# A decoder trunk on one core: one embedding projected later, one transposed earlier

## The chip, the cores and the metric
The kernel runs on one NeuronCore of a Trainium2 chip. The metric is the device time of one execution in microseconds (us). The kernel before takes 2688.65 us, the median of three timed runs (2688.11 to 2694.91).

## The reference
The program computes a decoder trunk of two layers on 256 tokens of width 2048, in float32. Each layer ends with a small product of an embedding `p[i]` (256 tokens by 256) and a weight of 256 by 2048, which enters only in the layer's last line:

```python
for i in range(DEPTH):                       # DEPTH = 2
    mix = ...                                # even: RWKV-7 and window attention; odd: differential attention
    x = layer_norm(alpha * x + mix, ln1_g[i], ln1_b[i])                                # first norm
    x = layer_norm(alpha * x + swiglu(x, ffn_w1[i], ffn_w3[i], ffn_w2[i]), ln2_g[i], ln2_b[i])  # second norm
    x = x + jax.nn.sigmoid(x @ ple_w_gate[i]) * (p[i] @ ple_w_proj[i])
```

So the product of `p[i]` and `ple_w_proj[i]` depends on nothing that the layer computes, and it may be done at any time before the gate is applied.

## The kernel before
The 256 tokens lie in two tiles of 128 rows (`x[0]`, `x[1]`), each 128 by 2048. A product is kept near float32 accuracy by splitting both factors in a high and a low half (`hi`/`lo` of a weight, `x0h`/`x0l` and so on of the activations) and adding three matmuls of 128x128 by 128x512: high by high (line 133), high by low (134), low by high (135).

`gemm` makes 512 columns of a product: two accumulators, one for each token tile, each a PSUM bank from the pool `mm` of four. Its weights come from `split_weights`: SP's queue loads 128x2x512 (512 KB, `raw`, four buffers), ACT makes `hi` (line 109), DVE makes `lo` (line 110); there are six `hi`/`lo` slots after `more()`. One such weight tile feeds 12 matmuls: two halves, three terms, two token tiles. A full product over x has eight weight tiles and 96 matmuls; the argument `head=HEAD` lets the first four tiles of a product run for the first token tile before they run for the second.

A norm is `ln_finish`. For each of four column groups (c) and both token tiles (t), DVE normalises in two operations (lines 221 and 223), PE transposes four blocks of 128x128 into a PSUM tile of the pool `sm` (line 229, in two pairs), and ACT and DVE split each pair in halves (lines 176 and 177) into `x0h`, `x0l`, ..., `x7l`. The FFN (`ffn`) follows a first norm: in two parts (six and five groups of 512 columns) it makes the products with w1 and w3, SiLU and transposes, and then the product with w2. `ple` follows a second norm: the gate's product, the sigmoid, and the sum.

The embedding goes through `embed` (load p), `embed_t` (transpose to `pTh`, `pTl`, by `split_t`, lines 170, 176, 177) and `project` (product with `ple_w_proj`, four groups of 512 columns, of one weight tile and 12 matmuls each, copied to `pj` by ACT in line 291). Before the change each layer projects groups 0 and 1 behind its first norm and groups 2 and 3 behind its second. The buffers of p and of pT are single, so those of layer 1 reuse those of layer 0.

The order in which an engine runs its instructions is fixed when the kernel is built, and it isn't the order of the code: the framework's scheduler moves an instruction ahead of others on its engine. An engine then runs its row strictly as it stands there, and waits at an instruction whose inputs are missing.

Of the kernel before, what the change touches and what calls it, by code (L numbers as in the profile page):

```python
# [47 lines left out]
class Trunk:  # L48
# [195 lines left out]
                nc.vector.bn_stats(out=st[t][:, c], in_=xc)  # L244


    def ffn(self, x, xT, w1, w3, w2):
        nc = self.nc
        st = self.ln_start()
        with self.tc.tile_pool(name="ffn", bufs=1) as fp:  # L250
            k0 = 0
            for part, chunks in enumerate((range(0, 6), range(6, 11))):
                gT = []
                for c in chunks:
                    h1 = self.gemm(xT, w1, c * 512, head=HEAD if c == 0 else 0)
                    sl = []
                    for t in range(NT):
                        s = fp.tile([P, 512], F32, name="silu", bufs=3)
                        nc.scalar.activation(out=s, in_=h1[t], func=AF.Silu)
                        sl.append(s)  # L260
                    h3 = self.gemm(xT, w3, c * 512)
                    for t in range(NT):
                        nc.vector.tensor_tensor(out=sl[t], in0=sl[t], in1=h3[t], op=ALU.mult)
                    for j in range(2):
                        gT.append(self.split_t([sl[t][:, j * 256:(j + 1) * 256] for t in range(NT)],
                                               f"g{len(gT)}", fp))
                for c in range(4):
                    acc = self.gemm(gT, w2, c * 512, rows=range(k0, k0 + 2 * len(gT), 2),
                                    tail=TAIL if part == 1 and c == 3 else 0)
                    self.residual(x, acc, c, st, first=part == 0, last=part == 1)  # L270
                k0 += 2 * len(gT)
        return st


    def embed(self, p):

        pt = []
        for t in range(NT):
            pc = self.ep.tile([P, PLE], F32, name=f"p{t}")
            self.nc.sync.dma_start(out=pc, in_=p[t * P:(t + 1) * P])  # L280
            pt.append(pc)
        return pt

    def embed_t(self, pt):
        return [self.split_t(pt, "pT", self.ep)]

    def project(self, pT, wpj, chunks, pj):
# [71 lines left out]
def kview(w):  # L359
    return w.rearrange("(ko p) n -> p ko n", p=P)  # L360
# [637 lines left out]
@with_exitstack  # L998
def decoder_trunk(ctx: ExitStack, tc: tile.TileContext, out, stop=None, **a):
    nc = tc.nc  # L1000
    T = Trunk(ctx, tc)
    T.ident = T.cp.tile([P, P], F32, name="ident")
    make_identity(nc, T.ident)
    T.mhalf = T.const("mhalf", [P, 4], -0.5)
    T.ninf = T.const("ninf", [P, 1], -3e38)

    def dump(x):
        for t in range(NT):
            nc.sync.dma_start(out=out[0, t * P:(t + 1) * P], in_=x[t])

    for i in range(DEPTH):
        p, wpj = a["p"][i, 0], kview(a["ple_w_proj"][i])
        if i % 2 == 0:
            x, st = even_layer(T, a, a["x"][0])
            T.more()
            T.ln_begin(a["ln1_g"][i], a["ln1_b"][i])
            pt = T.embed(p)
            banks = T.psum(4, 4)
        else:
            banks = T.psum(4, 4)  # L1020
            xT = T.transpose_x(x)
            T.ln_begin(a["ln1_g"][i], a["ln1_b"][i])
            pt = T.embed(p)
            st = odd_layer(T, x, xT, a, i)
        with tc.tile_pool(name="pj", bufs=1) as jp:
            pj = [jp.tile([P, D], F32, name=f"pj{t}") for t in range(NT)]
            xT = T.ln_finish(x, st)
            T.ln_begin(a["ln2_g"][i], a["ln2_b"][i])
            if stop == (i, 1):
                banks.close()  # L1030
                return dump(x)
            pT = T.embed_t(pt)
            T.project(pT, wpj, (0, 1), pj)
            st = T.ffn(x, xT, kview(a["ffn_w1"][i]), kview(a["ffn_w3"][i]), kview(a["ffn_w2"][i]))
            xT = T.ln_finish(x, st)
            if stop == (i, 2):
                banks.close()
                return dump(x)
            T.project(pT, wpj, (2, 3), pj)
            T.ple(x, xT, pj, kview(a["ple_w_gate"][i]), out[0] if i == DEPTH - 1 else None)  # L1040
        banks.close()
        if stop == (i, 3):
            return dump(x)
# [20 lines left out]
```

## Time and profile before

| | us |
|---|---|
| median of three timed runs | 2688.65 |
| lowest, highest | 2688.11, 2694.91 |
| the profiled execution | 2683.93 |
| its span, first to last instruction | 2682.2 |
| PE busy in it | 2595.9 (97%) |
| DVE, ACT busy | 1494.3, 1142.2 |
| granted TensorE clock, mean | 0.977 |

The granted clock is a share of 2.4 GHz, and 0.50 is the lower level of 1.2 GHz. PE is TensorE's matmul row, PEld its weight loads. Lines are those of the kernel before. The matmuls overlap at their ends, so the distance from one start to the next says what one costs.

### The profile page before, as it was taken

How to read it: one execution, taken by the hardware profiler on the slowest of the kernel's cores; microseconds unless marked ns; L12 is line 12 of the kernel's file. 1: busy time of each engine (PE TensorE's matmuls, PEld its weight loads, DVE VectorE, ACT ScalarE, POOL GpSimd, SP SyncE). 2: the span in 40 equal slices, each digit the busy share in tenths (PEclk: the TensorE clock that was granted, in tenths of full speed). 3: DMA queues.
4: the chain of work that ended last, by engine and by line, in shares of the span. 5: the costliest groups of instructions: out<-in, count | busy, mean ns of one | idle time of the engine just before them, and what ended most of it. 6: DMA issues, size and time to landing. Idle time of an engine off the chain costs nothing.

```text
span 2682.2 us, 32574 instructions
## 1 busy us (share of the span) xinstructions
PE 2595.9 (97%) x12509; PEld 2101.7 (78%) x12509; DVE 1494.3 (56%) x2072; ACT 1142.2 (43%) x1493; POOL 122.8 (5%) x190
## 2 busy tenths in 40 slices
PE   8998799989999999999999999998999999999999
PEld 6877566768888888888788777786888888888877
DVE  4769536674545444545666555555545444545574
ACT  5443224544444334444444454444444434444343
POOL 0113421000000000000000000000000000000000
PEclk9989889989999999999999999998999999999999
DMA  6335312556666666666575555555666666666654
GB/s 189 110 108 149 95 40 78 174 168 201 188 189 188 195 191 192 188 190 190 173 226 180 163 158 165 166 183 154 188 190 188 192 191 194 189 189 188 195 175 164
DMA packets 240282, 458.56 MB, mean 171 GB/s; under 512 B 15280, under 2 KB 20066, under 8 KB 240126
## 3 DMA queue, kind: packets, MB, share of 16 engines
q1 hardware_dynamic: 240126, 456.48, 56.4%
q8 instruction: 98, 1.61, 0.2%
q14 instruction: 58, 0.48, 0.1%
HBM read 453.28 MB, written 2.10 MB: 170 GB/s over the span
## 4 chain that ended last, share of the span: by engine, by line
PE 88%; DVE 6%; POOL 2%; DMA 2%; ACT 1%; issue 1%; SPq 0%; POOLq 0%; ACTq 0%; DVEq 0%
PE acc L133 26%; PE acc L134 25%; PE acc L135 25%; DVE lo L110 1%; PE acc L155 1%; PE acc L159 1%; PE acc L157 1%; PE s L170 1%; PE s L229 1%; DMA raw<-in_e_w_in_dram 1%; PE sx L861 1%; ACT hi L109 1%; DVE blk L609 0%; PE s L730 0%; DVE lmat L708 0%
## 5 line engine op out<-in xcount | busy, mean ns | idle before, releaser
L110 DVE TENSOR_TENSOR lo<-raw,hi 128x1024 fp32r<-128x1024 f32 (+2 forms) x840 | 1023.6, 1220 | 990.3 <-ACT hi L109 987.7
L109 ACT CAST hi<-raw 128x1024 fp32r<-128x1024 f32 (+2 forms) x840 | 879.0, 1047 | 1215.0 <-PE acc L135 1095.2
L133 PE MATMUL acc<-hi,x0h 128*128 128x512 f32 (+1 forms) x292 | 119.1, 408 | 0.3 <-ACT x0h L176 0.3
L134 PE MATMUL acc<-lo,x3h 128*128 128x512 f32 (+1 forms) x292 | 114.9, 394 | 4.3 <-DVE lo L110 4.3
L135 PE MATMUL acc<-hi,x0l 128*128 128x512 f32 (+1 forms) x292 | 117.3, 402 | 0.0
L134 PE MATMUL acc<-lo,x2h 128*128 128x512 f32 (+1 forms) x292 | 114.9, 393 | 2.3 <-DVE lo L110 2.3
L133 PE MATMUL acc<-hi,x1h 128*128 128x512 f32 (+1 forms) x292 | 116.9, 400 | 0.0
L134 PE MATMUL acc<-lo,x6h 128*128 128x512 f32 (+1 forms) x292 | 114.2, 391 | 2.2 <-DVE lo L110 2.2
L134 PE MATMUL acc<-lo,x4h 128*128 128x512 f32 (+1 forms) x292 | 114.5, 392 | 1.4 <-DVE lo L110 1.4
L135 PE MATMUL acc<-hi,x1l 128*128 128x512 f32 (+1 forms) x292 | 115.8, 396 | 0.0
L134 PE MATMUL acc<-lo,x1h 128*128 128x512 f32 (+1 forms) x292 | 115.7, 396 | 0.0
L133 PE MATMUL acc<-hi,x4h 128*128 128x512 f32 (+1 forms) x292 | 114.4, 392 | 1.2 <-DVE x L242 1.2
L134 PE MATMUL acc<-lo,x0h 128*128 128x512 f32 (+1 forms) x292 | 115.5, 396 | 0.0
L133 PE MATMUL acc<-hi,x2h 128*128 128x512 f32 (+1 forms) x292 | 115.3, 395 | 0.0
L133 PE MATMUL acc<-hi,x3h 128*128 128x512 f32 (+1 forms) x292 | 115.0, 394 | 0.0
L134 PE MATMUL acc<-lo,x5h 128*128 128x512 f32 (+1 forms) x292 | 114.1, 391 | 0.8 <-DVE lo L110 0.8
L135 PE MATMUL acc<-hi,x3l 128*128 128x512 f32 (+1 forms) x292 | 114.8, 393 | 0.0
L135 PE MATMUL acc<-hi,x7l 128*128 128x512 f32 (+1 forms) x292 | 114.7, 393 | 0.0
L135 PE MATMUL acc<-hi,x2l 128*128 128x512 f32 (+1 forms) x292 | 114.7, 393 | 0.0
L134 PE MATMUL acc<-lo,x7h 128*128 128x512 f32 (+1 forms) x292 | 114.6, 393 | 0.0
L133 PE MATMUL acc<-hi,x7h 128*128 128x512 f32 (+1 forms) x292 | 114.1, 391 | 0.0
L133 PE MATMUL acc<-hi,x6h 128*128 128x512 f32 (+1 forms) x292 | 113.9, 390 | 0.0
(561 smaller groups left out, 5196.3 us busy)
## 6 DMA issues: line engine op xcount, KB each, us to landing
raw<-in_ffn_w_dram SPq DMA_DIRECT2D x528, 512.0 KB, 3.7
raw<-in_o_w_in_dram SPq DMA_DIRECT2D x96, 512.0 KB, 3.9
raw<-in_e_w_in_dram SPq DMA_DIRECT2D x64, 512.0 KB, 3.6
raw<-in_ple_w_gate_dram SPq DMA_DIRECT2D x64, 512.0 KB, 4.6
raw<-in_e_w_out_dram SPq DMA_DIRECT2D x32, 512.0 KB, 3.6
raw<-in_o_w_out_dram SPq DMA_DIRECT2D x32, 512.0 KB, 4.1
x<-in_x_dram SPq DMA_DIRECT2D x16, 256.0 KB, 5.1
lng<-in_ln_g_dram SPq DMA_DIRECT2D x16, 256.0 KB, 3.2
```

The costliest lines, as they stand in the source:

```text
L109: nc.scalar.copy(out=hi, in_=raw)
L110: nc.vector.tensor_tensor(out=lo, in0=raw, in1=hi.bitcast(F32), op=ALU.subtract)
L133: nc.tensor.matmul(o, xh[:, kk, s], hi[:, kk], start=k == 0, stop=False)
L134: nc.tensor.matmul(o, xh[:, kk, s], lo[:, kk], start=False, stop=False)
L135: nc.tensor.matmul(o, xl[:, kk, s], hi[:, kk], start=False, stop=k == 2 * n - 1)
L155: nc.tensor.matmul(o, hi[:, kk, fs], xh[:, kk], start=k == 0 and i % 2 == 0, stop=False, skip_group_check=True)
L157: nc.tensor.matmul(o, lo[:, kk, fs], xh[:, kk], start=False, stop=False, skip_group_check=True)
L159: nc.tensor.matmul(o, hi[:, kk, fs], xl[:, kk], start=False, stop=k == nk - 1, skip_group_check=True)
L170: nc.tensor.transpose(ps[:, kk, t * P:(t + 1) * P], src[t][:, kk * P:(kk + 1) * P], self.ident)
L229: nc.tensor.transpose(ps[:, 2 * j + kk], x[t][:, f:f + P], self.ident)
L861: nc.tensor.matmul(ps, qT[s, c, f % 4, t * P:(t + 1) * P], kT[c][s, 0:nk * P], start=True, stop=True)
```

## The change
`embed_t` is gone: `embed` now loads and transposes. Layer 0 calls it between the FFN's two parts, and projects all four groups behind its second norm and none behind its first. Layer 1 calls it at the layer's start, before the attention, and projects as before (0 and 1 behind the first norm, 2 and 3 behind the second).

```diff
-    def ffn(self, x, xT, w1, w3, w2):
+    def ffn(self, x, xT, w1, w3, w2, between=None):
...
                     self.residual(x, acc, c, st, first=part == 0, last=part == 1)
                 k0 += 2 * len(gT)
+                if part == 0 and between:
+                    between()
         return st
...
             pt.append(pc)
-        return pt
-
-    def embed_t(self, pt):
         return [self.split_t(pt, "pT", self.ep)]
...
         p, wpj = a["p"][i, 0], kview(a["ple_w_proj"][i])
+        pT = []
         if i % 2 == 0:
             x, st = even_layer(T, a, a["x"][0])
             T.more()
             T.ln_begin(a["ln1_g"][i], a["ln1_b"][i])
-            pt = T.embed(p)
             banks = T.psum(4, 4)
+            first, between = (), lambda: pT.extend(T.embed(p))
         else:
             banks = T.psum(4, 4)
             xT = T.transpose_x(x)
             T.ln_begin(a["ln1_g"][i], a["ln1_b"][i])
-            pt = T.embed(p)
+            pT.extend(T.embed(p))
             st = odd_layer(T, x, xT, a, i)
+            first, between = (0, 1), None
...
-            pT = T.embed_t(pt)
-            T.project(pT, wpj, (0, 1), pj)
-            st = T.ffn(x, xT, kview(a["ffn_w1"][i]), kview(a["ffn_w3"][i]), kview(a["ffn_w2"][i]))
+            T.project(pT, wpj, first, pj)
+            st = T.ffn(x, xT, kview(a["ffn_w1"][i]), kview(a["ffn_w3"][i]), kview(a["ffn_w2"][i]), between)
             xT = T.ln_finish(x, st)
...
-            T.project(pT, wpj, (2, 3), pj)
+            T.project(pT, wpj, range(len(first), 4), pj)
```

On PE at layer 0's first norm, the row before (x_4677 and x_4678 are the two token tiles, p_5029 and p_5031 the two tiles of p):

```order
L229 MATMUL s<-ident,x_4677 128x128 x4
L229 MATMUL s<-ident,x_4678 128x128 x4
L229 MATMUL s<-ident,x_4677 128x128 x4
L229 MATMUL s<-ident,x_4678 128x128 x2
L170 MATMUL s<-ident,p_5029 128x128 x2
L170 MATMUL s<-ident,p_5031 128x128 x2
L133 MATMUL acc<-hi,pTh 128x512
L134 MATMUL acc<-lo,pTh 128x512
L133 MATMUL acc<-hi,pTh 128x512
L229 MATMUL s<-ident,x_4678 128x128 x2
```

The same place in the row of the changed kernel, from the last matmul of the layer's output projection on:

```order
L135 MATMUL acc<-hi,x7l 128x512
L229 MATMUL s<-ident,x_4677 128x128 x2
L133 MATMUL acc<-hi,x0h 128x512
L134 MATMUL acc<-lo,x0h 128x512
L229 MATMUL s<-ident,x_4677 128x128 x2
L135 MATMUL acc<-hi,x0l 128x512
L229 MATMUL s<-ident,x_4678 128x128 x2
L133 MATMUL acc<-hi,x0h 128x512
```

Before, 30 of the 32 transposes and those of p stand ahead of the first projection matmul, and all FFN matmuls behind the projection. Now FFN matmuls stand between the transposes from the second row on, 54 of them ahead of the last transpose.

On PE at layer 1's first norm, the row before, from its last transposes on:

```order
L229 MATMUL s<-ident,x_4677 128x128 x4
L229 MATMUL s<-ident,x_4678 128x128 x2
L170 MATMUL s<-ident,p_11216 128x128 x2
L170 MATMUL s<-ident,p_11218 128x128 x2
L133 MATMUL acc<-hi,pTh 128x512
```

And the row of the changed kernel there, from the end of the output projection on (oT7 is the attention's last operand):

```order
L135 MATMUL acc<-hi,oT7l 128x512
L229 MATMUL s<-ident,x_4677 128x128 x2
L133 MATMUL acc<-hi,pTh 128x512
L134 MATMUL acc<-lo,pTh 128x512
L135 MATMUL acc<-hi,pTl 128x512
```

The transposes of p have left this place (they now stand among the layer's first matmuls), and the projection follows the first pair of transposes. Layer 0's second norm has the same beginning before and after, with 48 projection matmuls in place of 24.

On SP's queue, from layer 0's first norm to its second, the row before has this (p_11216 and p_11218 are layer 1's p):

```order
L280 DMA p_11216<-in_p_dram 128x256
L108 DMA raw<-in_ffn_w_dram 128x2x512
L280 DMA p_11218<-in_p_dram 128x256
L108 DMA raw<-in_ffn_w_dram 128x2x512 x257
L108 DMA raw<-in_ple_w_proj_dram 128x2x512 x2
L108 DMA raw<-in_ple_w_gate_dram 128x2x512 x7
```

And the changed kernel this:

```order
L108 DMA raw<-in_ffn_w_dram 128x2x512 x145
L282 DMA p_11216<-in_p_dram 128x256
L282 DMA p_11218<-in_p_dram 128x256
L108 DMA raw<-in_ffn_w_dram 128x2x512 x111
L108 DMA raw<-in_ple_w_proj_dram 128x2x512 x4
L108 DMA raw<-in_ple_w_gate_dram 128x2x512 x5
```

Layer 1's p moved behind 145 more FFN tiles (153 with the eight ahead of the norm's rows), and the two projection tiles of the first norm joined those of the second. Layer 0's p stands where it stood, among the output projection's weights.

## Rows read from the trace of the kernel before

**Rows 1.** The page, part 1: busy us, share of the span, instructions.
```profile
PE 2595.9 (97%) x12509; PEld 2101.7 (78%) x12509; DVE 1494.3 (56%) x2072; ACT 1142.2 (43%) x1493; POOL 122.8 (5%) x190
```

**Rows 2.** Windows, four norms: stretch, length, busy PE PEld DVE ACT POOL, clock, DMA, GB/s.
```profile
560.11:611.71 51.60, 40.17 (x157) 29.26 (x157) 33.90 (x56) 21.62 (x34) 1.47 (x2) 0.77 0.56 167
1318.81:1352.70 33.89, 32.09 (x154) 24.97 (x152) 27.80 (x46) 16.80 (x29) 0.72 (x1) 1.00 0.67 202
1819.25:1870.76 51.51, 39.94 (x158) 29.59 (x156) 31.67 (x49) 20.46 (x33) 0.55 (x1) 0.77 0.54 161
2577.90:2611.66 33.76, 32.25 (x154) 24.97 (x152) 28.72 (x47) 17.09 (x29) 0.72 (x1) 1.00 0.54 174
```

**Rows 3.** Waits of PE, layer 0's first norm: total us, times, longest.
```profile
PE s L229 <- DVE x L223: 3.5, 1, 3.5
```

**Rows 4.** Waits of PE, layer 0's second norm.
```profile
PE s L229 <- DVE x2l L177: 1.1, 1, 1.1
PE acc L134 <- DVE lo L110: 0.6, 1, 0.6
```

**Rows 5.** Windows: layer 0's first norm in slices, columns as in rows 2.
```profile
560.11:563.72 3.61, 0.16 (x2) 0.00 (x1) 3.61 (x9) 2.09 (x2) 0.73 (x1) 0.80 0.59 186
563.72:582.47 18.75, 10.77 (x34) 5.20 (x35) 17.03 (x37) 6.18 (x16) 0.73 (x1) 0.50 0.47 135
582.47:586.05 3.58, 3.58 (x10) 2.80 (x10) 2.23 (x3) 0.37 (x1) 0.00 (x0) 0.50 0.90 251
...
589.95:611.71 21.76, 21.76 (x97) 18.02 (x96) 10.31 (x9) 10.36 (x11) 0.00 (x0) 1.00 0.61 187
```

**Rows 6.** Timeline of PE, layer 0's first norm: start, us, what, idle before.
```profile
563.72 0.69 PE L229 MATMUL s<-ident,x 128*128 128x128 f32 x2 [3.45 <-DVE x L223]
...
582.47 0.79 PE L133 MATMUL acc<-hi,pTh 128*128 128x512 f32 x1 [0.68 <-ACT pTh L176]
583.06 0.63 PE L134 MATMUL acc<-lo,pTh 128*128 128x512 f32 x1
583.49 0.63 PE L133 MATMUL acc<-hi,pTh 128*128 128x512 f32 x1
...
589.95 0.39 PE L133 MATMUL acc<-hi,x0h 128*128 128x512 f32 x1
```

**Rows 7.** Timeline of PE, layer 1's first norm.
```profile
1849.00 0.39 PE L133 MATMUL acc<-hi,x0h 128*128 128x512 f32 x1
```

**Rows 8.** Timeline of DVE in the steady FFN.
```profile
972.48 1.23 DVE L110 TENSOR_TENSOR lo<-raw,hi 128x1024 fp32r<-128x1024 f32 x1 [1.49 <-ACT hi L109]
```

**Rows 9.** Timelines of ACT and DVE, layer 0's first norm.
```profile
564.45 0.37 ACT L176 CAST x0h<-s 128x256 fp32r<-128x256 f32 x1 [1.99 <-PE s L229]
579.39 0.74 DVE L223 SCALAR_TENSOR_TENSOR x<-x,rs,lnb 128x512 f32<-128x512 f32 x1
```

**Rows 10.** Groups by form, layer 0's second norm: count, busy us, mean ns, idle.
```profile
L110 DVE TENSOR_TENSOR lo<-raw,hi 128x1024 fp32r<-128x1024 f32 x11 | 13.3, 1216 | 4.3 <-ACT hi L109 4.2
L291 ACT COPY pj<-acc 128x512 f32<-128x512 f32 x4 | 2.4, 589 | 1.7 <-PE acc L135 1.7
```

**Rows 11.** Timeline of SP's queue: the loads of p.
```profile
448.36 1.18 SPq L280 DMA_DIRECT2D p<-in_p_dram  x2
581.40 0.33 SPq L280 DMA_DIRECT2D p<-in_p_dram  x1
```

**Rows 12.** Timelines of SP and PE where the FFN's second part begins.
```profile
987.34 0.37 SPq L108 DMA_DIRECT2D raw<-in_ffn_w_dram  x1
990.05 0.37 SPq L108 DMA_DIRECT2D raw<-in_ffn_w_dram  x1
987.51 0.39 PE L133 MATMUL acc<-hi,x0h 128*128 128x512 f32 x1
```

**Rows 13.** Windows for line 229 alone: PE, PEld, clock, layer 0's first norm.
```profile
563.72:582.47 18.75, 9.92 (x30) 4.34 (x30) 0.50 0.47 135
```

**Rows 14.** Timeline of DVE, the last split of layer 0's second norm.
```profile
1341.03 0.42 DVE L177 TENSOR_TENSOR x7l<-s,x7h 128x256 fp32r<-128x256 f32 x1
```

## The prediction, made before the changed kernel was timed
> **What bounds the kernel now.** I read the page first: TensorE (PE) is busy 97% of the 2682.2 us span [rows 1], so only time in which it waits, or runs at the lower of its two clock levels, can be won. The view of windows came next, over four stretches of the same build: from the last matmul before a norm to the end of the first product behind it [rows 2]. Each holds 24 projection matmuls, 32 transposes of x and the 96 matmuls of one product. The two second norms take 33.89 and 33.76 us at a granted clock of 1.00 (2.4 GHz); the two first norms take 51.60 and 51.51 us at a mean of 0.77. The reader is to see that equal work costs 17.7 us more at a first norm.
>
> The view of waits says why. In layer 0's first norm PE waits for VectorE (DVE) before one transpose after the other [rows 3]; in the second norm only 1.7 us of waits are left [rows 4]. Sliced, the first norm shows 3.61 us with nothing to do, 18.75 us in which 34 matmuls fill 10.77 us at 0.50 (1.2 GHz), 3.58 us of dense work still at 0.50, and then full speed [rows 5]. The timeline of PE shows transposes alone from 563.72, the transposes of p behind nearly all of them, the first projection matmul at 582.47 and the first FFN matmul at 589.95 [rows 6]. Order does this: pT is made behind all of the norm's transposes, and the FFN's accumulators come after the projection's four banks. Layer 1's first norm reads the same [rows 7].
>
> **Layer 1, first norm.** The transposes of p now stand at the layer's beginning, so the queue has 24 ready matmuls behind the first transpose of x, in the pattern of a second norm. That pattern is measured: 33.8 us [rows 2]. The weights in front are the same (two projection tiles, seven FFN tiles), the DVE work is the same, and the residual runs as long. I take 33.8 for 51.5: **-17.7 us**. The other end: new waits of 3 us, -14.7. Late next is the wait for a low half of the weights (0.6 us) that rows 4 shows.
>
> The four p transposes themselves move into dense stretches at full clock. At the 0.155 us that a transpose costs in company (worked out below) that is **+0.6 us** for each layer, between 0 and 1. Their conversions on ACT and DVE lie under matmuls: in the steady FFN DVE, the busier of the two, idles 1.49 us of every 2.7 [rows 8].
>
> **Layer 0, first norm.** No projection is left here. The FFN's first product takes the free banks at once and its matmuls stand between the transposes. Nothing before the first transpose changes, so PE again idles to 563.72, with the clock falling to 0.50. The first matmul needs x0h, cast at 564.45 in 0.37 [rows 9], so it starts at about 564.9. From there PE has 96 matmuls and 30 transposes. A matmul costs 21.76 / 96 = 0.227 [rows 5]; a transpose in company (33.89 - 1.7 of waits - 120 x 0.227) / 32 = 0.155 [rows 2, 4]. That is 21.8 + 4.6 = 26.4 us. VectorE's last normalised piece came at 579.39 + 0.74, and its last splits would follow by about 582 [rows 9]; by the new order 54 of the matmuls stand ahead of the last transpose, 12.3 + 4.6 = 16.9 us, so PE, not DVE, is last. To this come the low clock and waits. In rows 5 dense work ran 3.58 us at 0.50, which costs 1.8 us of full-speed work; the new start still waits for splits here and there, so I take 2.4 (0 to 3.6). Waits were 1.7 us with a filler [rows 4]; I take 1.5 (0 to 3). End: 564.9 + 26.4 + 2.4 + 1.5 = 595.2, against 611.71: **-16.5 us**, bounds 591.3 (-20.4) and 597.9 (-13.8).
>
> On the low clock the row speaks first: it stayed at 0.50 through the whole stretch from 563.72 to 582.47, in which PE ran transposes with a wait between one and the next [rows 5, 6]. The Trainium skill ("TensorE: Matmul & The Clock Gate", section "HAM oscillation — how this bites in real kernels") says that a stream of matmuls broken by long enough waits falls back to half rate and opens its next burst there, again at every such wait. The trace agrees that the grant falls where PE idles (a mean of 0.80 in the idle 3.61 us, 0.50 in the next 18.75). The rule speaks against taking the filler out of this norm: by it layer 0 would come out as in the first rival below, and by the row on dense work one cold start is paid.
>
> **Layer 0, second norm.** 24 more projection matmuls: 24 x 0.227 = 5.4 us. They may cover the 1.7 us of waits there, so 3.7; with a new wait of 1 us, 6.5. Part of those waits is for weights and norm rows, which a filler does not bring sooner: I take **+4.7 us**. Two more low halves (1.22 us each) and four more copies (0.59 each) [rows 10] fit: DVE was busy 27.80 and ACT 16.80 of 33.89 us [rows 2], and the stretch grows.
>
> **Queues.** Layer 0's p is still loaded at 448.36 [rows 11]. Layer 1's p loads, which were at 581.40 and just after, move on SP to behind the 153rd FFN weight tile. They reuse the buffer of layer 0's p and so add a wait for its transposes; behind them stand all weight loads. In the trace PE starts on the FFN's second part (145th tile) at 987.5 and a weight load is issued at 987.34, the next at 990.05 [rows 12]: one load per 2.7 us, each 9 tiles ahead of PE, so the 153rd is that one and the p transposes end at about 988. The wait is under 1 us and hidden; its cover is some 9 x 2.7 = 24 us of tiles.
>
> **Sum.** -17.7 + 0.6 + 0.6 - 16.5 + 4.7 = -28.3 us. The profiled execution took 2683.93 us (span 2682.2), so 2655.6; the median of the timed runs is 2688.65, 4.7 us above it, so **2660.3 us**. Adding ends: best -20.4 + 3.7 - 17.7 = -34.4 (2654.3), worst -13.8 + 1.0 + 1.0 + 6.5 - 14.7 = -20.0 (2668.7).
>
> **Rivals.** First: the clock in layer 0's first norm stays at 0.50 until the last transpose, as it did before. At that level a matmul comes every 0.43 us [rows 6] and a transpose takes 0.33 (30 in 9.92 us) [rows 13]. So 54 matmuls lose 0.20 each and 30 transposes 0.18: 16 us in place of 2.4, and the gain there is 3. Total -28.3 + 13.6 = -14.7: 2674.0. For it: the 3.61 us of idling is still there. Against it: at low clock PE's work per piece of 128 rows and 512 columns is 12 x 0.43 + 4 x 0.33 = 6.5 us, more than the 18.75 / 8 = 2.3 us in which DVE delivers one, so PE could not wait, and dense work brought the clock back in both first norms.
>
> Second: at layer 0's second norm four projection tiles hold four of six converted-weight slots, and the gate's third and fourth low halves fall behind the norm's work on DVE, which lasted to 1341.4 with two fewer [rows 14]; two halves of 1.22 and the extra 2.4 bring 1346. PE would have used up its ready work (48 projection, 24 gate matmuls, 26 transposes: 20.4 us from 1318.8) at 1339: a wait of 7 us. Total -21.3: 2667.4. Against it: in the new order two of these halves stand among the norm's operations, not behind them.
>
> Third, slower than before: the low clock outlives the norm. Each us of work at 0.50 costs half a us against full speed, so -28.3 is used up when the clock stays low for 57 us more than I take, and it would be slower by over 8 us from 73 us on, with most of the FFN's first w1 and w3 products at low clock: 2697 us or more. For it stands only that waits start it; against it, 21.76 us of the same product ran at 1.00 in rows 5 right after the dense work. At some 41 to 73 us it would read as no change.
>
> **How the numbers follow.** My forecast (2652 to 2670) has 0.82, the first rival 0.08, the second 0.04, a low clock that leaves no change 0.03, the slower one 0.03. The first two rivals are both faster, so faster by over 0.3% (8 us, about what a measurement of this kernel can tell from no change) has 0.94, same 0.03, slower 0.03. Range 2652 to 2675: from below the best sum to just past the first rival.
>
> **What would show it.** In the new profile: the stretch from layer 1's out-projection to the end of the FFN's first product near 34 us at a clock of 1.00, with projection matmuls right behind the first transposes; the same stretch in layer 0 near 35 us, with FFN matmuls between transposes and one low spell that ends some 5 us, at most 7, behind the first of them; layer 0's second norm near 38.6 us; the gate and FFN streams unchanged. I am wrong if the clock stays at 0.50 for more than 10 us in layer 0's first norm, if PE waits for low halves at its second norm for more than 2 us, or if any stall appears where the FFN's second part begins.

## The result and the profile after

The changed kernel takes **2654.54 us** (median of four runs, 2653.56 to 2654.94) against 2688.38 us (2687.68 to 2694.91) of the kernel before in the same session: a ratio of 0.9868, 95% interval 0.9851 to 0.9885, or 33.8 us less. The forecast was 2660.3, the range 2652 to 2675. The profiled execution of the changed kernel took 2654.55 us, its span 2652.9, at a mean granted clock of 0.983 (before 0.977).

PE has the same 12509 instructions as in [rows 1]; it is busy 2585.4 us, 10.5 less, and the span is 29.3 us shorter.

The same four stretches as in [rows 2], from the last matmul before a norm to the end of the first product behind it (length, then busy PE, PEld, DVE, ACT, POOL, the granted clock, the DMA share, GB/s):

```profile
563.12:595.77 32.65, 28.09 (x130) 21.49 (x130) 28.23 (x51) 13.71 (x24) 1.46 (x2) 0.95 0.57 180
1303.36:1340.81 37.45, 37.20 (x177) 29.56 (x176) 31.43 (x49) 21.07 (x36) 0.72 (x1) 1.00 0.68 221
1807.66:1841.32 33.66, 32.04 (x154) 25.02 (x152) 28.84 (x47) 17.08 (x29) 0.72 (x1) 1.00 0.68 207
2548.47:2582.30 33.83, 32.20 (x153) 24.96 (x152) 28.14 (x47) 17.09 (x29) 0.72 (x1) 1.00 0.56 174
```

Layer 0's first norm went from 51.60 to 32.65 us (-18.95), its second from 33.89 to 37.45 (+3.56), layer 1's first from 51.51 to 33.66 (-17.85), its second from 33.76 to 33.83. With 0.45 us for each layer's transposes of p (below) that is -32.3 us. The span differs by 29.3 only because everything ahead of the first stretch, which the change does not touch, ended at 563.12 in this execution and at 560.11 in the one before. In the timed runs the difference is 33.8.

In layer 0's first stretch PE idled 51.60 - 40.17 = 11.43 us before [rows 2] and 4.56 now. Its busy time fell by 12.08 us; 5.44 of these are the 24 projection matmuls that left, 0.6 the transposes of p, and the remaining 6 are work that no longer runs at the low clock. The waits of PE in the stretch, which answer to [rows 3] (total us, times, longest):

```profile
PE s L229 <- DVE x L223: 3.5, 1, 3.5
PE acc L134 <- DVE lo L110: 0.6, 1, 0.6
PE acc L133 <- ACT x0h L176: 0.5, 1, 0.5
```

The first of them is the idle stretch ahead of the first transpose, as before. Behind it the kernel before had these, where a transpose waits until DVE's split (line 177) of an earlier pair is done:

```profile
PE s L229 <- DVE x0l L177: 2.4, 2, 1.4
PE s L229 <- DVE x2l L177: 1.8, 2, 0.9
PE s L229 <- DVE x4l L177: 1.8, 2, 0.9
PE s L229 <- DVE x6l L177: 0.9, 1, 0.9
```

These waits between one transpose and the next are gone. The same stretch in slices, as [rows 5]:

```profile
563.12:566.74 3.62, 0.16 (x1) 0.00 (x1) 3.62 (x9) 2.08 (x2) 0.73 (x1) 1.00 0.58 181
566.74:568.00 1.26, 0.80 (x4) 0.50 (x4) 1.26 (x6) 0.37 (x1) 0.67 (x1) 0.98 0.93 291
568.00:571.40 3.40, 3.40 (x11) 2.49 (x10) 3.40 (x9) 0.75 (x2) 0.06 (x1) 0.50 0.26 93
571.40:595.77 24.37, 23.74 (x117) 18.50 (x116) 19.95 (x31) 10.51 (x19) 0.00 (x0) 1.00 0.59 186
```

The clock still falls to 0.50 (1.2 GHz), for 3.40 us of dense work; then all is at full speed (2.4 GHz). Before, the low clock lasted 18.75 us of broken work and 3.58 of dense. The timeline of PE at the beginning of the stretch, to be set beside [rows 6] (start, us, what, idle before it):

```profile
566.74 0.44 PE L229 MATMUL s<-ident,x 128*128 128x128 f32 x2 [3.46 <-DVE x L223]
567.64 0.55 PE L133 MATMUL acc<-hi,x0h 128*128 128x512 f32 x1 [0.46 <-ACT x0h L176]
567.99 0.63 PE L134 MATMUL acc<-lo,x0h 128*128 128x512 f32 x1
568.43 0.69 PE L229 MATMUL s<-ident,x 128*128 128x128 f32 x2
```

FFN matmuls stand behind the first pair of transposes, where before only transposes, of x and of p, followed until 582.47 [rows 6].

Where the FFN's second part begins, PE now transposes layer 0's p between two matmuls:

```profile
971.34 0.39 PE L135 MATMUL acc<-hi,g11l 128*128 128x512 f32 x1
971.57 0.60 PE L170 MATMUL s<-ident,p 128*128 128x128 f32 x4
971.92 0.48 PE L133 MATMUL acc<-hi,x0h 128*128 128x512 f32 x1
972.24 0.40 PE L134 MATMUL acc<-lo,x0h 128*128 128x512 f32 x1
```

From 971.34 to 972.24 two matmuls of 0.227 us and the four transposes start, so these cost 0.45 us; the same is taken for layer 1's. Layer 1's loads of p wait for them on SP's queue, between two issues of weights, in the timeline of SP there:

```profile
968.66 3.09 SPq L108 DMA_DIRECT2D raw<-in_ffn_w_dram  x2
971.98 0.81 SPq L282 DMA_DIRECT2D p<-in_p_dram  x2
974.11 0.38 SPq L108 DMA_DIRECT2D raw<-in_ffn_w_dram  x1
```

They are issued 0.4 us behind the start of the transposes, and PE shows no idle time there.

### The profile page after: what moved, and what is told of

The parts are those of the page before. It is cut to its first block, busy times and chain, and to the rows that moved or that the text cites. A ratio compares the mean times of both kernels' runs of the same rounds, so it can differ in the third digit from the quotient of the medians.

```text
span 2652.9 us, 32574 instructions
## 1 busy us (share of the span) xinstructions
PE 2585.4 (97%) x12509; PEld 2097.4 (79%) x12509; DVE 1492.6 (56%) x2072; ACT 1138.9 (43%) x1493; POOL 121.9 (5%) x190
## 4 chain that ended last, share of the span: by engine, by line
PE 88%; DVE 6%; POOL 2%; DMA 2%; ACT 1%; issue 1%; SPq 0%; ACTq 0%; POOLq 0%; DVEq 0%
PE acc L133 26%; PE acc L134 26%; PE acc L135 26%; DVE lo L110 2%; PE acc L155 1%; PE acc L159 1%; PE acc L157 1%; PE s L170 1%; PE sx L860 1%; ACT hi L109 1%; DVE blk L608 0%; PE s L729 0%; DVE lmat L707 0%; DMA lnb<-in_ln_b_dram 0%; PE s L934 0%
## 5 line engine op out<-in xcount | busy, mean ns | idle before, releaser
L135 PE MATMUL acc<-hi,x4l 128*128 128x512 f32 (+1 forms) x292 | 115.1, 394 | 0.0
L133 PE MATMUL acc<-hi,x5h 128*128 128x512 f32 (+1 forms) x292 | 114.1, 391 | 0.0
```

The lines of the kernel that those rows point to most:

```text
L133: nc.tensor.matmul(o, xh[:, kk, s], hi[:, kk], start=k == 0, stop=False)
L135: nc.tensor.matmul(o, xl[:, kk, s], hi[:, kk], start=False, stop=k == 2 * n - 1)
```

## The experiments

The first four of the eight ran beside the kernel before at 2688.62 us (13 runs, 2684.18 to 2695.29), the other four, the changed kernel again among them, beside it at 2690.05 (11 runs, 2686.36 to 2699.36). Each says what it changes against the kernel before or the changed one; `...` marks what is left out of an edit.

### One layer at a time

`e1_layer1_only` keeps layer 0 as before (late transposes, groups 0 and 1 at its first norm) and changes layer 1; `e2_layer0_only` does the reverse.

In both, `load_p` only loads p, and `turn_p` transposes it behind the norm, as before:

```diff
 # e1, against the changed kernel: layer 0
-            first, between = (), lambda: pT.extend(T.embed(p))
+            pt, first, between = T.load_p(p), (0, 1), None
...
+            if not pT:
+                pT.extend(T.turn_p(pt))
 # e2, against the changed kernel: layer 1
-            pT.extend(T.embed(p))
+            pt = T.load_p(p)
...
+            if not pT and pt:
+                pT.extend(T.turn_p(pt))
```

> Only layer 1's embedding is loaded and transposed at the layer's start; layer 0 is as before. Theory (each first norm lost its time by itself, because the transposes of p stood behind the norm's): layer 1's first norm takes 33.7 us in place of 51.5, its p transposes cost 0.45 elsewhere, nothing else moves: -17.4 us, 2671 us. Rival (what was won came mostly from layer 0 taking its projection out of the first norm): less than half of the 33.8 us, above 2672 us, and layer 1's first norm stays over 40 us. Second rival (the two parts help each other): the parts alone sum to clearly less than the whole.

> Only layer 0 is changed (p transposed between the FFN's parts, no projection at the first norm, four groups at the second); layer 1 is as before. Theory: first norm 51.6 to 32.7, second norm 33.9 to 37.5, p transposes +0.45: -14.9 us, 2673.5 us; with the layer 1 part -32.3. Rival: the first norm needs the projection as ready work, and without layer 1's part the gain is under 10 us.

Measured: e1 2672.35 us (2670.68 to 2673.28), ratio 0.9942 [0.9927, 0.9957], -16.3 us; e2 2674.48 (2669.47 to 2677.42), 0.9948 [0.9934, 0.9963], -14.1 us. The first norms of the two layers in e1 (windows, columns as above):

```profile
564.78:616.15 51.37, 39.64 (x157) 29.00 (x157) 33.97 (x56) 21.64 (x35) 1.46 (x2) 0.80 0.56 168
1823.67:1856.94 33.27, 32.23 (x154) 24.98 (x152) 29.34 (x47) 17.06 (x29) 0.72 (x1) 1.00 0.70 213
```

Layer 0's first and second norm and layer 1's first in e2:

```profile
564.27:598.25 33.98, 28.98 (x129) 22.35 (x129) 28.85 (x51) 14.30 (x25) 1.46 (x2) 0.90 0.58 179
1305.83:1344.35 38.52, 37.31 (x178) 29.58 (x176) 31.55 (x49) 20.80 (x35) 0.73 (x1) 1.00 0.64 214
1810.66:1862.38 51.72, 40.12 (x158) 29.73 (x157) 31.79 (x49) 20.47 (x33) 0.55 (x1) 0.77 0.53 161
```

Each norm is short where it was changed and 51 to 52 us where it was not. The two gains add to 30.4 us against 33.8 for both: two separate gains, of about equal size. Each interval is about 4 us wide to either side, so whether the two parts also help each other by some 3 us stays open. The rival for e1 had named a time above 2672 us and a norm above 40 us; the time is just past its mark, but the norm fell to 33.27, so what e1 gained is layer 1's own.

### Is it the early transposes, or what is queued in front?

`e3_late_none_first` transposes p late, as before, in both layers, and only moves the projection: none at the first norm, four groups at the second. `e5_late_one_first` transposes late too and leaves one group (two accumulators of the pool's four) at the first norm.

```diff
 # e3, against the kernel before
-            T.project(pT, wpj, (0, 1), pj)
...
-            T.project(pT, wpj, (2, 3), pj)
+            T.project(pT, wpj, range(4), pj)
 # e5, against the kernel before
-            T.project(pT, wpj, (0, 1), pj)
+            T.project(pT, wpj, (0,), pj)
...
-            T.project(pT, wpj, (2, 3), pj)
+            T.project(pT, wpj, (1, 2, 3), pj)
```

> p is transposed where it was before, behind the norm's own transposes, in both layers; but neither layer projects at its first norm, both project all four groups at the second. Theory (the projection kept the FFN's matmuls from going between the transposes; with none of it there the place of the p transposes does not matter): per layer 51.6 to about 33.1 at the first norm and 33.8 to 37.5 at the second: -29.5 us, 2659 us. Rival (what counts is that p is transposed a stage earlier): nothing of that is done here, so the first norms stay above 45 us and the time above 2683 us.

> As before, with the p transposes late, but one group of the projection (two accumulators of four) at each first norm and three at each second. Theory as the prediction put it (late pT, and the four banks of the projection that keep the FFN out): two banks are free for the FFN here; but in the built row the FFN's matmuls still stand behind the projection and all transposes before it, so the first norm only loses the 12 matmuls (some of them at the low clock): 47 to 48.5 us, the second gains 1.8 to 2.7: -2 to -3 us in all for both layers, 2685 to 2687. Rival (the banks alone were the cause): the first norm falls to 33 to 38 us and the time to 2660 or less.

Measured: e3 2654.82 us (2651.3 to 2659.09), ratio 0.9883 [0.9866, 0.9899], -33.8 us, as much as the whole change. Layer 0's two norms and layer 1's first in e3:

```profile
559.03:591.92 32.89, 28.56 (x133) 21.97 (x133) 28.93 (x52) 14.51 (x26) 1.46 (x2) 0.95 0.59 187
1298.99:1336.52 37.53, 37.11 (x178) 29.71 (x177) 31.34 (x49) 20.82 (x35) 0.72 (x1) 1.00 0.71 225
1802.92:1834.04 31.12, 28.44 (x133) 22.38 (x132) 26.99 (x46) 14.18 (x25) 0.55 (x1) 0.95 0.67 201
```

Transposing early is not what counts: without it, the first norms are short as soon as no projection stands at them. Moving the projection is enough for the whole gain.

e5 took 2684.73 us (ten runs, 2677.4 to 2694.2), ratio 0.9985 [0.9972, 0.9999]. Its first norms stay long (49.94 and 48.93 us, where 47 to 48.5 had been expected), and its second ones hardly grow (by 0.3 us, where 1.8 to 2.7 had been expected). Layer 0's first and second norm:

```profile
567.71:617.65 49.94, 38.35 (x145) 27.72 (x145) 32.60 (x55) 19.52 (x31) 1.46 (x2) 0.76 0.53 162
1324.77:1358.91 34.14, 34.14 (x165) 27.49 (x164) 30.20 (x48) 18.87 (x32) 0.72 (x1) 1.00 0.67 220
```

The timeline of PE in e5's first norm of layer 0:

```profile
571.25 0.44 PE L229 MATMUL s<-ident,x 128*128 128x128 f32 x2 [3.39 <-DVE x L223]
572.94 1.14 PE L229 MATMUL s<-ident,x 128*128 128x128 f32 x4 [1.25 <-DVE x0l L177]
...
587.05 1.41 PE L229 MATMUL s<-ident,x 128*128 128x128 f32 x4 [0.92 <-DVE x6l L177]
588.26 1.06 PE L170 MATMUL s<-ident,p 128*128 128x128 f32 x4
589.99 0.79 PE L133 MATMUL acc<-hi,pTh 128*128 128x512 f32 x1 [0.68 <-ACT pTh L176]
```

PE still runs transposes alone for 17 us, although only two of the four accumulators are the projection's. In e5 FFN matmuls mix with those of the projection (the first starts at 592.29), but none goes ahead of the first one at 589.99. So the account of the four banks in the prediction does not hold for the stretch that costs the time: half as many banks in use, and the FFN's matmuls stay out of the norm's transposes all the same.

### The order of the code alone

`e7_project_behind_h1` keeps everything of the kernel before (late transposes, two groups at each norm) except that the code calls the first two groups behind the FFN's first product rather than ahead of it.

```diff
...
                     h1 = self.gemm(xT, w1, c * 512, head=HEAD if c == 0 else 0)
+                    if c == 0:
+                        behind()
...
-            T.project(pT, wpj, (0, 1), pj)
-            st = T.ffn(x, xT, kview(a["ffn_w1"][i]), kview(a["ffn_w3"][i]), kview(a["ffn_w2"][i]))
+            st = T.ffn(x, xT, kview(a["ffn_w1"][i]), kview(a["ffn_w3"][i]), kview(a["ffn_w2"][i]),
+                       lambda: T.project(pT, wpj, (0, 1), pj))
```

> As before (p transposed late, two groups of the projection at the first norm and two at the second), but the code calls the first two groups behind the FFN's first product instead of ahead of it. Nothing is transposed a stage earlier. Theory (the projection held the FFN only because it stood ahead of it in the code while its input came last): FFN matmuls go between the transposes, the first norm to the end of the first product takes 32.9 us plus 0.5 for p, the 24 projection matmuls follow at full clock for 5.4: 38.5 in place of 51.5, second norm 33.8 as before: -26 us for both layers, 2662 us. Rival (the p transposes a stage ahead are needed): first norms above 45 us, above 2680 us.

Measured: 2659.52 us (2658.66 to 2663.7), ratio 0.989 [0.9876, 0.9904], -30.5 us. The first norms, with their 24 projection matmuls at the end, in windows of e7:

```profile
563.42:601.33 37.91, 33.78 (x157) 26.51 (x157) 31.16 (x54) 19.57 (x32) 1.46 (x2) 0.95 0.61 201
1808.99:1845.57 36.58, 33.91 (x158) 26.80 (x156) 28.59 (x48) 18.08 (x31) 0.55 (x1) 0.95 0.65 201
```

And PE at layer 0's first norm in e7:

```profile
567.05 0.44 PE L229 MATMUL s<-ident,x 128*128 128x128 f32 x2 [3.47 <-DVE x L223]
567.95 0.80 PE L133 MATMUL acc<-hi,x0h 128*128 128x512 f32 x1 [0.46 <-ACT x0h L176]
```

The transposes of p still stand late, at 584.26. The same matmuls, transposes and banks at the same norm: 51.60 [rows 2] becomes 37.91 us by moving one call behind another. What held the FFN back was a product called ahead of it whose input is made last in the norm. Early transposes make that input ready, and leaving the projection out takes the product away; each removes the cause. The 24 projection matmuls of e7 run densely behind the product and cost their full price there, 5.4 us at each first norm. The changed kernel, which ran beside e7 and in which they are cheaper (below), took 2654.29 us, 5.2 less.

### Is the filler worth anything?

The filler is what stands between a norm's transposes besides the product that follows: here the projection matmuls. `e8_no_filler` projects all four groups of both layers between the FFN's two parts, in the dense stream, and none at any norm; `e4_early_split` transposes early in both layers and puts two groups at each norm. The changed kernel ran again beside them.

```diff
 # e8, against the kernel before: both layers transpose p ahead of the first norm
...
-            st = T.ffn(x, xT, kview(a["ffn_w1"][i]), kview(a["ffn_w3"][i]), kview(a["ffn_w2"][i]))
+            st = T.ffn(x, xT, kview(a["ffn_w1"][i]), kview(a["ffn_w3"][i]), kview(a["ffn_w2"][i]),
+                       lambda: T.project(pT, wpj, range(4), pj))
...
-            T.project(pT, wpj, (2, 3), pj)
 # e4, against the changed kernel: layer 0
-            first, between = (), lambda: pT.extend(T.embed(p))
+            pT.extend(T.embed(p))
+            first, between = (0, 1), None
```

> All four groups of both projections run between the FFN's two parts, at full clock and in the dense stream; no projection at any norm. Theory: both norms take 31 to 33 us each, and the 48 matmuls of a layer cost 10.9 us where they now stand: per layer 64 + 10.9 + 0.45, against 70.1 + 0.45 in layer 0 and 67.5 + 0.45 in layer 1 of the changed kernel: 5 to 13 us slower than it, 2660 to 2668 us. So much the filler is worth. Rival (a norm without ready projection matmuls goes back to over 45 us): 2690 us or more.

> Both embeddings are transposed ahead of their layer's first norm (layer 0's at the end of its mixer), and both layers project two groups at each norm. Theory (ready projection matmuls between a norm's transposes cost next to nothing, 24 of them at each norm is where most of them hide): layer 0's first norm 33.7 us or a little less, since matmuls stand even ahead of its first transpose, and its second 33.9; together 67.5 against 70.1 in the changed kernel: 2.5 us faster than it, about 2652 us. Rival (layer 0 cannot transpose p that early, or its place among the output projection's matmuls costs as much): the same time as the changed kernel or more, 2655 us or above.

> The changed kernel once more, on the chip of the three others, as their yardstick: 2654.5 us, stretches of 32.7 and 37.5 us in layer 0, 33.7 and 33.8 in layer 1.

Measured: the changed kernel again 2654.29 us (2650.84 to 2657.08), ratio 0.9866 [0.9852, 0.9881]. e8 took 2663.17 (2661.42 to 2666.53), 0.9903 [0.9887, 0.9919], 8.9 us more than the changed kernel. Its four norms in windows:

```profile
563.14:595.76 32.62, 27.98 (x129) 21.63 (x129) 28.62 (x52) 14.44 (x25) 1.46 (x2) 0.95 0.61 184
1313.62:1343.98 30.36, 26.88 (x130) 20.69 (x129) 25.97 (x45) 13.06 (x24) 0.55 (x1) 1.00 0.65 207
1810.96:1841.19 30.23, 26.93 (x129) 20.58 (x128) 26.06 (x45) 13.09 (x24) 0.55 (x1) 1.00 0.70 206
2559.13:2589.92 30.79, 26.84 (x129) 20.66 (x128) 25.37 (x44) 12.37 (x23) 0.55 (x1) 1.00 0.54 168
```

Without any filler a norm takes 30.2 to 32.6 us and not 51: the product that follows the norm fills the gaps between the transposes by itself. The filler can only be worth about what PE still idles in these windows (30.36 - 26.88 = 3.5 us at layer 0's second norm). In the dense stream 96 projection matmuls cost 96 x 0.227 = 21.8 us; in the changed kernel they add 37.45 - 30.36, 33.66 - 30.23 and 33.83 - 30.79, together 13.6 us. So 48 matmuls at one norm saved 3.8 us of their price and 24 saved 2.0 and 2.4. The difference, 8.2, is nearly all of the 8.9 measured.

e4 took 2659.14 us (six runs, 2654.4 to 2674.38), ratio 0.9893 [0.9871, 0.9914], no better than the changed kernel, where some 2 us less had been expected; the time lies where its rival had put it. Its three later stretches take 33.4 to 34.2 us, as they should; layer 0's first norm takes 39.66 where 33.7 was expected. The whole stretch and four slices of it:

```profile
565.82:605.48 39.66, 35.27 (x153) 27.03 (x152) 32.75 (x55) 20.07 (x33) 1.46 (x2) 0.91 0.61 195
565.82:569.79 3.97, 1.75 (x9) 1.16 (x7) 3.97 (x10) 2.80 (x4) 0.73 (x1) 1.00 0.62 212
569.79:573.50 3.71, 3.71 (x14) 2.92 (x14) 3.06 (x10) 1.43 (x4) 0.73 (x1) 0.57 0.38 129
586.00:588.00 2.00, 0.90 (x5) 0.45 (x5) 2.00 (x4) 0.74 (x2) 0.00 (x0) 0.84 0.34 128
588.00:590.00 2.00, 2.00 (x5) 1.51 (x6) 1.70 (x3) 0.00 (x0) 0.00 (x0) 0.50 0.58 166
```

Layer 0 can transpose p that early: seven projection matmuls stand ahead of the first transpose, right behind the output projection, and are used up at 567.4 us. The timeline of PE:

```profile
565.82 0.39 PE L133 MATMUL acc<-hi,pTh 128*128 128x512 f32 x1
...
569.79 0.41 PE L229 MATMUL s<-ident,x 128*128 128x128 f32 x2 [2.21 <-DVE x L223]
...
587.95 0.80 PE L134 MATMUL acc<-lo,x2h 128*128 128x512 f32 x1 [0.63 <-DVE lo L110]
```

PE idles 2.21 us in place of 3.46, and the clock falls all the same. The last projection matmul starts at 575.90. Later PE runs out of work again (0.90 of 2.00 us busy) and the clock falls a second time: from 584.08 on only transposes stand in the row, which wait for DVE, until the next FFN matmul gets the low half of its weights. That filler kept for this hole would have closed it is likely, but no run shows it.

## Why the prediction was right, step by step

- **What bounds it** held: the gain is PE's waits between transposes and the low clock that went with them, in the two first norms alone. One sentence of that part failed: "the FFN's accumulators come after the projection's four banks". With two banks in use (e5) the stretch stayed at 49.94 us; with four in use but the code's order turned (e7) it fell to 37.91. The order of the calls, with pT made last, is the cause. The terms of the sum came from measured stretches and from the prices of matmuls and transposes, and none depended on that sentence.
- **Layer 1, first norm:** -17.7 said, -17.85 measured. Taking the second norm's measured pattern for it was right, and none of the 3 us of new waits came.
- **Transposes of p:** +0.6 said for each layer, +0.45 measured at layer 0's and not measured by itself at layer 1's.
- **Layer 0, first norm:** -16.5 said, -18.95 measured, inside the bounds. From the first FFN matmul to the end 30.3 us were forecast (26.4 of work, 2.4 for the low clock, 1.5 of waits); it took 595.77 - 567.64 = 28.13. The low clock lasted 3.40 us, which costs 1.7; one wait of 0.6 came; the remaining 25.8 are work. Each of the three was taken 0.6 to 0.9 too large, and the first FFN matmul came 0.3 us sooner behind the first transpose than said. One step did not follow from its own sum: 564.9 + 16.9 = 581.8 against DVE's end at about 582 leaves open which of the two is last; only with the low clock added is it PE. It held: behind the first transpose none waits for DVE in the profile.
- **Layer 0, second norm:** +4.7 said, +3.56 measured, just outside the lower bound of 3.7. The bound let the filler cover at most the 1.7 us of waits; PE's idle time in the stretch was 33.89 - 32.09 = 1.80 [rows 2] and is now 37.45 - 37.20 = 0.25. The waits for low halves and norm rows, which were to stay, were covered too.
- **Queues:** as said. The loads of p stand between two weight loads and no stall followed.
- **The sum:** -28.3 said, -32.3 in the profiled execution; 2.45 of the difference is layer 0's first norm, 1.1 its second, 0.3 the transposes. The other part of the 5.8 us between 2660.3 and 2654.54 is the step from one execution to the median: before, the profiled run lay 4.7 us under the median and after it lies on it, while its beginning, unchanged, took 3.0 us longer. The misses at the norms all lie on one side: 2654.54 is just above the best sum, 2654.3, and 2.5 us above the lower end of the range.
- **The rivals:** the first needed the clock at 0.50 until the last transpose. It was low from 568.0 to 571.4 and at 1.00 from there on, so dense work brings it back as the prediction argued. The rule of the Trainium skill that it weighed ("TensorE: Matmul & The Clock Gate", section "HAM oscillation — how this bites in real kernels") is borne out by e4, where the clock fell twice, each time where PE ran out of work. In e5 the trace shows one fall, behind 3.39 us of idling, and then a mean clock of 0.52 over the 18.74 us from the first transpose to the first projection matmul, with waits of 0.68 to 1.37 us. At this norm of the changed kernel the first idling took the clock down once and no further wait did, since the FFN's matmuls took the filler's place. The second rival's 7 us wait at layer 0's second norm did not come: PE idles 0.25 us there. Nor did the clock stay low beyond the norm. That filler is worth little where the next product can fill (e8) had no place among the rivals.

Not settled: why the row that was built for e5 lets no FFN matmul ahead of the first projection matmul when two accumulators are free. e7 shows which order of the calls cures it, not by which rule the scheduler decides.

## What to carry to other kernels

Where an engine runs transposes alone and waits between them, look in its row for the product that stands first behind them and ask when its input is made: one small product whose input comes last can hold back a large one that is ready in pieces. Calling it later, or making its input earlier, cures this; adding filler is worth only the idle time that is then left. A stretch of the same build that does not show the stall (here the second norm, 33.76 and 33.89 us) gives the price of the cured one: layer 1's first norm took 33.66 us, and 33.27 (e1) and 33.32 (the changed kernel again).

## What the runs showed of the hardware beyond that

- The same 3.6 us of idling at layer 0's first norm took the clock down at different moments: in the execution before it was already at a mean of 0.80 within the idle time [rows 5], in the one after at 1.00 within it and at 0.50 only from 568.00, when two transposes and the first FFN matmul had started. In e2, the same code as the changed kernel at this norm, the mean was 0.90 and the stretch 33.98 us against 0.95 and 32.65: PE idled 0.45 us longer ahead of the first transpose (3.91 in place of 3.46), and its busy time, at the lower mean clock, was 0.89 us longer (28.98 and 28.09). So the price of a single cold start differs by about 1 us from run to run.
- Filler in a norm stretch does not cost in proportion. At a clock of 1.00 throughout, the stretch took 30.2 to 30.8, 33.3 to 34.4, 34.1 and 37.4 to 38.5 us with 0, 24, 36 and 48 projection matmuls: the third dozen (e5's second norms) costs next to nothing and uses up the last idle time of PE (34.14 busy of 34.14 us); the fourth costs at least its full price, 12 x 0.227 = 2.7 us.
- The unchanged part ahead of layer 0's first norm ended between 559.03 (e3) and 567.71 us (e5) in the profiled executions. No edit here explains these 8.7 us; their cause stays open, and they are a fourth of the gain, so the stretches were compared and not the spans.
